# Recurrent mixer: block sums of the weights by accumulating transfers, and heads 0 to 3 scaled in earlier scans

## The chip, the cores and the metric

The kernel runs on one core of one Trainium2 chip. Five engines share the core: TensorE (PE in the profile; PEld is its loading of stationary operands), VectorE (DVE), ScalarE (ACT), GpSimd (POOL) and SyncE (SP), which here only issues transfers. The metric is the device time of one execution in microseconds (us). Before the change it is 2783.34 us, the median of three runs from 2783.18 to 2783.43.

## The reference, cut to what matters

The program is a trunk of two layers over 768 tokens (two requests, 512 and 256 long) with 1024 features, all in fp32. Each layer is `x += 1/2 ffn(norm(x)); x += mixer(norm(x)); x += 1/2 ffn(norm(x))`. The mixer of the first layer is the recurrent one that the change touches; the second layer's is windowed attention. The recurrent mixer, cut to its core:

```python
def hgrn2_mixer(x, w_in, w_o, g_norm, lb):
    q, i, g, f_fw, f_bw = jnp.split(x @ w_in, 5, axis=-1)      # 8 heads of 128
    k_f, logf_f = gates(f_fw, lb[0])
    k_b, logf_b = gates(f_bw, lb[1])
    o_fwd = gla_chunk_scan(q, k_f, i, logf_f)   # S_t = diag(f_t) S_(t-1) + k_t v_t^T, o_t = S_t^T q_t
    o_bwd = rev(gla_chunk_scan(rev(q), rev(k_b), rev(i), rev(logf_b)))
    o = o_fwd + o_bwd
    o = o * lax.rsqrt(jnp.mean(o * o, axis=-1, keepdims=True) + NORM_EPS)   # per head and token
    o = (o * g_norm).reshape(B, T, H * V) * jax.nn.silu(g)
    return o @ w_o
```

Three of its matrix products have 1024 by 1024 weights and matter here: the values `i` ("v"), the gate `g` ("g") and the output product with `w_o` ("o").

## The kernel before, in words

**Products in three parts.** Every fp32 matrix is split into a high and a low half that TensorE can take at its faster type: `hi` is a cast of the value (ACT), `lo` is the value less `hi` (DVE). A product is then three matmuls, hi·hi, hi·lo and lo·hi. A split of a weight thus costs one cast on ACT and one subtraction on DVE (`split`, L175 and L323/L324).

**Block products.** Each of v, g and o is computed as seven products of blocks in place of eight, a scheme of the Strassen kind. The token side gives `b00`, `b10`, `b11` and four mixed factors `t1` to `t4` (`mix`, L418ff: block sums on DVE, L426 to L432). The weight is cut into quarters a11, a12, a21, a22, and needs these sums: a21 += a22, a11 += a21 (called "second"), a12 += a11 ("fourth"), and s3, which is the a21 as loaded plus a11. Product p1 uses a11 as loaded, p2 uses a12 as loaded, p3 the summed a12, p4 a22, p5 the summed a21, p6 the summed a11, and p7 s3. `tok_steps` (L223ff) loads the quarters by the SP queue and makes them ready. A quarter is held in two halves, kp 0 (one tile `wr` of 128x1024) and kp 1 (two tiles `tA` of 128x512). s3 and a21 += a22 are made by `into` (L147), an accumulating transfer on GpSimd's queue, which adds one tile onto another without a compute engine. "second" and "fourth" are `tensor_add`s on DVE, three for each sum (one of 128x1024, two of 128x512). For v and g, whose products come in the order `TOK` = p1, p2, p7, p6, p5, p4, p3, these adds stand ahead of the splits of p6 and p3 (L260); for o, in the order `OUT` = p1, p2, p3, p7, p6, p4, p5, both stand behind the split of p2 (L272). They are pinned to the program's order.

**Stages.** After the first feed-forward part come the value block (542 to 600 us in the trace), eight scans of one head each (about 42 us each, 600 to 938), the rest of the gate block (to 967) and the output block (to 1029). A scan (`hgrn_scan`, L829ff) goes through seven levels. At each one ACT copies the keys into an operand (`kop`, L857), PE makes the score matmuls from it (`scan_scores`, L827), and DVE writes the scores under a mask (L844 to L846) and updates queries and keys (L879, L883). At its end the head's outputs are copied to the value tiles and their sums of squares kept (L932 to L938). `weave` (L715) puts pieces of other PE work between the steps of a scan: chunks of the next heads' projections (evacuated by ACT at L803) and then products of the gate block (L764 is the matmul of all three block products).

**The normalisation.** `rstds` takes a square root on ACT (L1030) and a reciprocal on DVE. The square root is in another table of ACT than its other functions, so ACT loads a table ahead of it and again behind it. `scaled` then multiplies a head's six blocks of 128x128 by these numbers, on ACT (L1078). Before the change `rstds(0, 7)` runs once, when seven scans are done, and the seven heads are scaled during the eighth scan, one head at each level.

**The start of the output block.** `gated` multiplies the scaled outputs by the gate; `turned` transposes them; `mix` makes t1 to t4 from them, and each operand is split by a cast on ACT and a subtraction on DVE. The product p3 of o is evacuated by a copy on ACT (L1140), into tiles that p7 needs; x is loaded back meanwhile, and p2 is added to it on DVE (L1147).

**What sets the order.** The program is written against a tile scheduler. It puts each engine's instructions into a fixed order by its own model of times, unless they are pinned; every engine then takes its list in order, and waits at an instruction whose inputs or buffers are not ready. Eight `w` tiles hold split weights, four `wr` and eight `tA` raw ones, and PSUM has eight banks. A split is started when buffers come free, so its place among PE's products is set by them.

Of the kernel before, what the change touches and what calls it, by code (L numbers as in the profile page):

```python
# [25 lines left out]
HEADS = 8  # L26
# [18 lines left out]
TOK = ("p1", "p2", "p7", "p6", "p5", "p4", "p3")  # L45
TCHAIN = {"p2": "p1", "p4": "p5", "p3": "p7"}
OUT = ("p1", "p2", "p3", "p7", "p6", "p4", "p5")
# [5 lines left out]
class Trunk:  # L53
# [174 lines left out]
    def tok_steps(self, key, srcs, order):  # L228
        nc = self.nc
        flat = lambda t: t.rearrange("p a b -> p (a b)")  # L230

        def fetch(src):
            t = self.wp.tile([P, 1024], F32, tag="wr", name=self.name("wr"), bufs=RAWBUFS)
            nc.sync.dma_start(t.rearrange("p (a b) -> p a b", a=2), src[0])
            parts = [[t], [self.tmp(512), self.tmp(512)]]
            for a, t in enumerate(parts[1]):
                self.last_load = nc.sync.dma_start(t, src[1][:, a, :])
            return parts

        a11, a12, a21, a22 = (fetch(src) for src in srcs)  # L240
        more = self.big([P, 2, 512])
        s3 = [
            [self.wp.tile([P, 512], F32, tag="s3", name=self.name("s3"), bufs=2) for _ in range(2)],
            [more[:, a, :] for a in range(2)],
        ]
        for kp in range(2):
            for a, t in enumerate(s3[kp]):
                self.last_load = nc.sync.dma_start(t, srcs[2][kp][:, a, :])
                self.into(t, a11[0][0][:, a * 512 : (a + 1) * 512] if kp == 0 else a11[1][a])
            for t, u in zip(a21[kp], a22[kp]):  # L250
                self.into(t, u)
        own = {"p1": a11, "p2": a12, "p3": a12, "p4": a22, "p5": a21, "p6": a11, "p7": s3}
        second, fourth = (a11, a21), (a12, a11)
        sums = {"p6": (second,), "p3": (fourth,)} if order == TOK else {}
        behind = {"p2": (second, fourth)} if order == OUT else {}

        def step(name, kp):
            for total, part in sums.get(name, ()):
                for t, u in zip(total[kp], part[kp]):
                    self.tc.keep_in_program_order(nc.vector.tensor_add(t, t, u))  # L260
            hi, lo = self.wtile(), self.wtile()
            at = 0
            for src in own[name][kp]:
                n = src.shape[-1]
                h, l = (t[:, at : at + n] for t in (hi, lo))
                self.split(src, h, l)
                at += n
            view = lambda t: t.rearrange("p (a b) -> p a b", a=2)
            self.staged[(*key, name, kp)] = (view(hi), view(lo), 2)
            for total, part in behind.get(name, ()):  # L270
                for t, u in zip(total[kp], part[kp]):
                    self.tc.keep_in_program_order(nc.vector.tensor_add(t, t, u))  # L272

        return [(2, lambda name=name, kp=kp: step(name, kp)) for name in order for kp in range(2)]

    def stage_next(self):
# [698 lines left out]
    def hgrn(self, lb_row, gn_row, next_row):  # L975
        nc = self.nc
# [4 lines left out]
        heads = [{} for _ in range(HEADS)]  # L981
# [35 lines left out]
        scan = lambda hd: self.hgrn_scan(hd, vs)  # L1017

        def stream():
            for h in range(1, HEADS):  # L1020
                for c in (0, 3, 4):
                    if (h, c) not in LEAD:
                        yield from self.hgrn_chunk(h, heads[h], c, range(2))
                self.hgrn_gates(h, heads[h])
# [3 lines left out]
        def rstds(a, b):  # L1028
            r = rs[:, a:b, :]
            nc.scalar.activation(r, self.hss[:, a:b, :], AF.Sqrt, bias=self.eps, scale=1.0 / P)  # L1030
            nc.vector.reciprocal(r, r)
# [42 lines left out]
        def scaled(first, last):  # L1074
            for b in range(NBLK):
                for h in range(first, last):
                    u = vs[b][:, h * P : (h + 1) * P]
                    nc.scalar.activation(u, u, AF.Copy, scale=rs[:, h, b : b + 1])  # L1078
# [21 lines left out]
        def gate():  # L1100
            need = {"p1": "t3", "p2": "t2", "p7": "t1", "p6": "t4"}
            for at in self.tok_quad(("g",), TOK, TCHAIN, self.ops, evac_g):
                if at[1:] == (HB - 1, 1) and at[0] in need:
                    self.reload_factor(need[at[0]])
                yield at

        feed = itertools.chain(stream(), gate())
        for h in range(HEADS - 1):
            self.weave(scan(heads[h]), feed, 16 if h == 0 else 18)
        rstds(0, HEADS - 1)  # L1110
        self.weave(scan(heads[-1]), feed, 20, also=lambda i: i < HEADS - 1 and scaled(i, i + 1))
        rstds(HEADS - 1, HEADS)
        scaled(HEADS - 1, HEADS)
        for i in range(HB):
# [441 lines left out]
```

## Time and profile before

| | |
|---|---|
| median of 3 runs | 2783.34 us (2783.18 to 2783.43) |
| the profiled execution | 2783.55 us |
| its span, first to last instruction | 2781.6 us |
| mean granted TensorE clock | 0.998 |
| value block, 542.4 to 599.6 us: PE busy | 57.20 of 57.20 |
| scans one to seven, 599.6 to 892.0: PE busy | 291.94 of 292.40 |
| eighth scan, 892.0 to 938.0: PE busy | 43.10 of 46.00 |
| gate block's rest, 938.0 to 967.5: PE busy | 29.50 of 29.50 |
| output block, 967.5 to 1029.0: PE busy | 58.26 of 61.50 |

The stages' rows are from the view that cuts the span into windows. The difference between a window's length and PE's busy time is PE's waiting; busy time at a lower granted clock still counts as busy. Groups of instructions are named by line, engine, operation and tiles (out<-in); the number in brackets behind an instruction is how long its engine stood idle ahead of it, and on whom it waited.

### The profile page before, as it was taken

How to read it: one execution, taken by the hardware profiler on the slowest of the kernel's cores; microseconds unless marked ns; L12 is line 12 of the kernel's file. 1: busy time of each engine (PE TensorE's matmuls, PEld its weight loads, DVE VectorE, ACT ScalarE, POOL GpSimd, SP SyncE). 2: the span in 40 equal slices, each digit the busy share in tenths (PEclk: the TensorE clock that was granted, in tenths of full speed). 3: DMA queues.
4: the chain of work that ended last, by engine and by line, in shares of the span. 5: the costliest groups of instructions: out<-in, count | busy, mean ns of one | idle time of the engine just before them, and what ended most of it. 6: DMA issues, size and time to landing. Idle time of an engine off the chain costs nothing.

```text
span 2781.6 us, 40766 instructions
## 1 busy us (share of the span) xinstructions
PE 2750.1 (99%) x15117; PEld 2555.3 (92%) x15117; DVE 2228.3 (80%) x3825; ACT 1387.6 (50%) x2586; POOL 393.9 (14%) x431
## 2 busy tenths in 40 slices
PE   8999999999999999999999999999999999999998
PEld 8999999989999879999999999999888889999998
DVE  8788788777887888788878887887848878788877
ACT  7344443634445765444445543444458855444443
POOL 2111121100000001211111121111102211211111
PEclk9999999999999999999999999999999999999999
DMA  6554554731121533655444355544422123655443
GB/s 173 128 126 117 126 141 123 244 107 39 39 67 50 173 92 81 147 133 129 117 113 119 81 144 134 124 122 114 129 73 76 45 63 75 146 133 129 117 115 107
DMA packets 337351, 313.41 MB, mean 113 GB/s; under 512 B 12584, under 2 KB 258816, under 8 KB 337152
## 3 DMA queue, kind: packets, MB, share of 16 engines
q1 hardware_dynamic: 296992, 221.81, 27.1%
q0 software_dynamic: 35856, 75.51, 15.0%
q10 hardware_dynamic: 4304, 13.49, 1.3%
q8 instruction: 119, 1.95, 0.3%
q14 instruction: 80, 0.66, 0.1%
HBM read 225.82 MB, written 15.73 MB: 87 GB/s over the span
## 4 chain that ended last, share of the span: by engine, by line
PE 95%; DVE 2%; ACT 2%; DMA 0%; issue 0%; DVEq 0%; ACTq 0%
PE ps L517 42%; PE ps L581 21%; PE ps L319 6%; PE ps L318 6%; PE ps L320 6%; PE ps L764 5%; PE ps L827 3%; PE ps L932 1%; PE ps L1418 1%; PE ps L908 1%; PE ps L389 1%; PE ps L1430 0%; PE ps L1380 0%; PE ps L1381 0%; PE ps L1431 0%; PE ps L1181 0%
## 5 line engine op out<-in xcount | busy, mean ns | idle before, releaser
L517 PE MATMUL ps<-big,w 128*128 128x384 f32 x6720 | 1169.3, 334 | 0.0
L517 PEld LDWEIGHTS ps<-big,w 128*128 128x128 f32 x6720 | 1165.9, 188 | 1.7 <-ACT tA L534 0.2
L208 ACT CAST w<-wr 128x512 fp32r<-128x512 f32 x600 | 416.0, 707 | 682.6 <-PE ps L517 274.2
L581 PE MATMUL ps<-w,big 128*128 128x512 f32 x2520 | 575.6, 389 | 0.0
L581 PEld LDWEIGHTS ps<-w,big 128*128 128x128 f32 x2520 | 472.6, 188 | 97.9 <-DVE x L603 0.3
L209 DVE TENSOR_TENSOR w<-wr,w 128x512 fp32r<-128x512 f32 (+1 forms) x520 | 430.3, 831 | 156.6 <-ACT w L208 140.1
L603 DVE SCALAR_TENSOR_TENSOR x<-ps,x 128x512 f32<-128x512 f32 x468 | 301.9, 683 | 10.1 <-PE ps L320 10.0
L147 POOL DMA_DIRECT2D s<-wr x126 | 110.9, 885 | 1353.5 <-DMA s<-in_ffn_w_dram 410.0
L318 PE MATMUL ps<-big,w 128*128 128x384 f32 x640 | 219.3, 345 | 2.0 <-ACT w L175 1.0
L319 PE MATMUL ps<-big,w 128*128 128x384 f32 x640 | 215.5, 337 | 0.9 <-DVE big L324 0.9
L320 PE MATMUL ps<-big,w 128*128 128x384 f32 x640 | 214.5, 335 | 0.0
L323 ACT CAST big<-tA 128x384 fp32r<-128x384 f32 x296 | 148.0, 513 | 114.3 <-DVE tA L549 36.4
L764 PE MATMUL ps<-w,big 128*128 128x512 f32 x756 | 179.7, 395 | 3.2 <-ACT big L1140 2.6
L764 PEld LDWEIGHTS ps<-w,big 128*128 128x128 f32 x756 | 141.4, 189 | 33.5 <-ACT big L1140 3.5
L324 DVE TENSOR_TENSOR big<-tA,big 128x384 fp32r<-128x384 f32 x296 | 166.2, 572 | 6.6 <-ACT big L323 4.5
L209 POOL TENSOR_TENSOR w<-wr,w 128x512 fp32r<-128x512 f32 x80 | 136.0, 1700 | 187.2 <-ACT w L208 182.8
L147 POOL DMA_DIRECT2D wr<-wr x103 | 90.8, 882 | 459.5 <-DMA wr<-in_ffn_w_dram 175.3
L318 PE MATMUL ps<-w,big 128*128 128x512 f32 x336 | 134.7, 401 | 0.3 <-DVE big L1441 0.2
L215 DVE TENSOR_TENSOR wr<-wr,wr 128x512 f32<-128x512 f32 (+1 forms) x120 | 122.9, 1024 | 14.2 <-issue 10.2
L320 PE MATMUL ps<-w,big 128*128 128x512 f32 x336 | 132.2, 393 | 0.5 <-DVE big L404 0.5
L319 PE MATMUL ps<-w,big 128*128 128x512 f32 x336 | 131.6, 392 | 0.0
L318 PEld LDWEIGHTS ps<-big,w 128*128 128x128 f32 x640 | 119.9, 188 | 3.2 <-ACT w L175 1.3
(219 smaller groups left out, 3471.2 us busy)
## 6 DMA issues: line engine op xcount, KB each, us to landing
wr<-in_ffn_w_dram SPq DMA_DIRECT2D x264, 512.0 KB, 4.0
s<-wr POOLq DMA_DIRECT2D x126, 256.0 KB, 4.9
s<-in_ffn_w_dram SPq DMA_DIRECT2D x120, 256.0 KB, 3.3
wr<-wr POOLq DMA_DIRECT2D x80, 256.0 KB, 3.8
wr<-in_hg_w_in_dram SPq DMA_DIRECT2D x32, 512.0 KB, 3.9
wr<-wr POOLq DMA_DIRECT2D x23, 512.0 KB, 4.6
spill<-x ACTq DMA_DIRECT2D x12, 512.0 KB, 3.9
kept<-big POOLq DMA_DIRECT2D x8, 768.0 KB, 5.4
```

What stands on the lines that cost most here:

```text
L147: self.nc.gpsimd.dma_start(out, src, accum_op=ALU.add)
L208: nc.scalar.copy(h, src)
L209: (eng or nc.vector).tensor_sub(l, src, h.bitcast(F32))
L318: nc.tensor.matmul(out, a[0], b[0], start=first, stop=False)
L319: nc.tensor.matmul(out, a[0], b[1], start=False, stop=False)
L320: nc.tensor.matmul(out, a[1], b[0], start=False, stop=last)
L323: self.nc.scalar.copy(hi, src)
L324: self.nc.vector.tensor_sub(lo, src, hi.bitcast(F32))
L517: self.nc.tensor.matmul(ps, a[x], b[y], start=first and k == 0 and i == 0, stop=k == 3 and i == 2, skip_group_check=True,)
L581: nc.tensor.matmul(ps, a[x], w[y], start=name == chain and kp == 0 and q == 0, stop=kp == 1 and q == 2, skip_group_check=True,)
L603: self.nc.vector.scalar_tensor_tensor(x, ps, c, x, ALU.mult, ALU.add)
L764: nc.tensor.matmul(ps, x[:, sl], y, start=fresh and k == 0 and q == 0, stop=k == 3 and q == 2, skip_group_check=True,)
```

## The change

First, "second" and "fourth" are no longer added on DVE. They become accumulating transfers on GpSimd's queue, for v, g and o alike: a11 += a21 is issued behind the split of p1, and a12 += a11 behind the split of p2, half by half. For o the quarters are also loaded in another order, a21 and a22 ahead of a11 and a12. In all 18 additions on DVE (six for each block product) become 18 transfers.

Second, the normalisation is cut in three. `rstds(0, 4)` runs when four scans are done, and heads 0 to 3 are to be scaled at the levels 1 and 4 of the scans behind it, one head at a time. `rstds(4, 7)` runs when seven are done, and the eighth scan scales heads 4 to 6 only, at its levels 1, 3 and 5. This makes one square root and two table loads more.

```diff
--- before.py
+++ after.py
@@ -237,7 +237,8 @@
                 self.last_load = nc.sync.dma_start(t, src[1][:, a, :])
             return parts
 
-        a11, a12, a21, a22 = (fetch(src) for src in srcs)
+        got = {i: fetch(srcs[i]) for i in ((0, 1, 2, 3) if order == TOK else (2, 3, 0, 1))}
+        a11, a12, a21, a22 = (got[i] for i in range(4))
         more = self.big([P, 2, 512])
         s3 = [
             [self.wp.tile([P, 512], F32, tag="s3", name=self.name("s3"), bufs=2) for _ in range(2)],
@@ -250,14 +251,9 @@
             for t, u in zip(a21[kp], a22[kp]):
                 self.into(t, u)
         own = {"p1": a11, "p2": a12, "p3": a12, "p4": a22, "p5": a21, "p6": a11, "p7": s3}
-        second, fourth = (a11, a21), (a12, a11)
-        sums = {"p6": (second,), "p3": (fourth,)} if order == TOK else {}
-        behind = {"p2": (second, fourth)} if order == OUT else {}
+        behind = {"p1": (a11, a21), "p2": (a12, a11)}
 
         def step(name, kp):
-            for total, part in sums.get(name, ()):
-                for t, u in zip(total[kp], part[kp]):
-                    self.tc.keep_in_program_order(nc.vector.tensor_add(t, t, u))
             hi, lo = self.wtile(), self.wtile()
             at = 0
             for src in own[name][kp]:
@@ -267,9 +263,9 @@
                 at += n
             view = lambda t: t.rearrange("p (a b) -> p a b", a=2)
             self.staged[(*key, name, kp)] = (view(hi), view(lo), 2)
-            for total, part in behind.get(name, ()):
-                for t, u in zip(total[kp], part[kp]):
-                    self.tc.keep_in_program_order(nc.vector.tensor_add(t, t, u))
+            if name in behind:
+                for t, u in zip(*(parts[kp] for parts in behind[name])):
+                    self.into(t, u)
 
         return [(2, lambda name=name, kp=kp: step(name, kp)) for name in order for kp in range(2)]
 
@@ -1106,9 +1102,13 @@
 
         feed = itertools.chain(stream(), gate())
         for h in range(HEADS - 1):
-            self.weave(scan(heads[h]), feed, 16 if h == 0 else 18)
-        rstds(0, HEADS - 1)
-        self.weave(scan(heads[-1]), feed, 20, also=lambda i: i < HEADS - 1 and scaled(i, i + 1))
+            early = (lambda i, h=h: i in (1, 4) and len(ready) and scaled(*ready.pop(0))) if h > 3 else None
+            self.weave(scan(heads[h]), feed, 16 if h == 0 else 18, also=early)
+            if h == 3:
+                rstds(0, 4)
+                ready = [(i, i + 1) for i in range(4)]
+        rstds(4, HEADS - 1)
+        self.weave(scan(heads[-1]), feed, 20, also=lambda i: i in (1, 3, 5) and scaled(4 + i // 2, 5 + i // 2))
         rstds(HEADS - 1, HEADS)
         scaled(HEADS - 1, HEADS)
         for i in range(HB):
```

Below are rows of the engines' orders. A row names the line, the operation and its tiles; the lines of the changed kernel are four lower than those of the kernel before in this part of the code. Names: L938 and L934 are the copies of a head's outputs into the value tiles x, L857 and L853 the key copies, L1078 and L1074 the scalings, `hrs` the reciprocal roots, `ps` a PSUM bank.

ACT at the end of the fourth scan and the start of the fifth, before:

```order
L936 ACTIVATE big_6810<-ps_6859 128x256
L938 COPY x_5093<-ps_6859 128x128
L938 COPY x_5109<-ps_6859 128x128
L857 COPY big_6884<-big_6781 128x768
L175 CAST w_6929<-wr_6401 128x1024
L803 ACTIVATE big_6789<-ps_6848 128x384
```

and after:

```order
L934 COPY x_5115<-ps_6859 128x128
L1026 ACT_TABLE_LOAD
L1026 ACTIVATE hrs<-hss,eps 128x24
L853 COPY big_6886<-big_6781 128x768
L1074 ACTIVATE x_5082<-x_5082,hrs 128x128
L1074 ACTIVATE x_5098<-x_5098,hrs 128x128
L1074 ACTIVATE x_5114<-x_5114,hrs 128x128
L1074 ACTIVATE x_5083<-x_5083,hrs 128x128
L1074 ACTIVATE x_5099<-x_5099,hrs 128x128
L1074 ACTIVATE x_5115<-x_5115,hrs 128x128
```

The square root and its table load now stand between the copies of the fourth head's outputs and the second key copy of the fifth scan, and six scalings follow that copy; all 24 scalings of heads 0 to 3, and the load of the other table, stand in this scan.

ACT in the eighth scan, around the key copy of its fifth level, before:

```order
L1078 ACTIVATE x_5109<-x_5109,hrs 128x128
L1078 ACTIVATE x_5076<-x_5076,hrs 128x128
L1078 ACTIVATE x_5092<-x_5092,hrs 128x128
L1078 ACTIVATE x_5108<-x_5108,hrs 128x128
L857 COPY big_7990<-big_7893 128x768
L1078 ACTIVATE x_5077<-x_5077,hrs 128x128
L1078 ACTIVATE x_5093<-x_5093,hrs 128x128
L323 CAST w_8183<-tA_7395 128x512
```

and after (L1041 evacuates a product of the gate block, L319 and L323 are casts of weights for it):

```order
L319 CAST w_8157<-wr_7413 128x1024
L1074 ACTIVATE x_5082<-x_5082,hrs 128x128
L319 CAST w_8200<-tA_7415 128x512
L1041 ACTIVATE big_8108<-ps_8051 128x512
L319 CAST w_8200<-tA_7416 128x512
L1074 ACTIVATE x_5098<-x_5098,hrs 128x128
L853 COPY big_8022<-big_7925 128x768
L1074 ACTIVATE x_5114<-x_5114,hrs 128x128
L1074 ACTIVATE x_5083<-x_5083,hrs 128x128
```

Ahead of this key copy there stood a run of scalings; now there are casts of weights, with two scalings among them and two behind.

DVE at the start of the output block, before (L324 are splits of weights, L272 the additions "second" and "fourth", L426 and L427 the first block sums, L1147 an addition of p2 to x):

```order
L324 TENSOR_TENSOR w_8709<-wr_8314,w_8708 128x1024
L272 TENSOR_TENSOR wr_8308<-wr_8308,wr_8320 128x1024
L324 TENSOR_TENSOR w_8715<-tA_8316,w_8714 128x512
L272 TENSOR_TENSOR wr_8314<-wr_8314,wr_8308 128x1024
L324 TENSOR_TENSOR w_8715<-tA_8317,w_8714 128x512
L272 TENSOR_TENSOR tA_8310<-tA_8310,tA_8322 128x512
L272 TENSOR_TENSOR tA_8311<-tA_8311,tA_8323 128x512
L272 TENSOR_TENSOR tA_8316<-tA_8316,tA_8310 128x512
L272 TENSOR_TENSOR tA_8317<-tA_8317,tA_8311 128x512
L426 TENSOR_TENSOR big_8577<-big_8746,big_8577 128x768
L1147 TENSOR_TENSOR x_8678<-ps_8724,x_8678 128x512
L427 TENSOR_TENSOR big_8746<-big_8481,big_8746 128x768
```

and after:

```order
L320 TENSOR_TENSOR w_8714<-wr_8331,w_8713 128x1024
L320 TENSOR_TENSOR w_8719<-tA_8333,w_8718 128x512
L320 TENSOR_TENSOR w_8719<-tA_8334,w_8718 128x512
L422 TENSOR_TENSOR big_8579<-big_8748,big_8579 128x768 x2
L423 TENSOR_TENSOR big_8748<-big_8486,big_8748 128x768 x2
L426 TENSOR_TENSOR big_8486<-big_8486,big_8579 128x768 x2
L428 TENSOR_TENSOR big_8656<-big_8656,big_8486 128x768
L1147 TENSOR_TENSOR x_8683<-ps_8726,x_8683 128x512
```

The six additions are gone from between the splits of p2 (its a12 as loaded is `wr_8314`, `tA_8316`, `tA_8317` before and `wr_8331`, `tA_8333`, `tA_8334` after), and the block sums follow the last of these splits directly. The additions are found again on POOL, as the last transfers of the mixer:

```order
L147 DMA wr_8325<-wr_8313 128x1024
L147 DMA tA_8327<-tA_8315 128x512
L147 DMA tA_8328<-tA_8316 128x512
L147 DMA wr_8331<-wr_8325 128x1024
L147 DMA tA_8333<-tA_8327 128x512
L147 DMA tA_8334<-tA_8328 128x512
```

In these `wr_8325`, `tA_8327` and `tA_8328` are a11, to which a21 is added; `wr_8331`, `tA_8333` and `tA_8334` are a12, to which that sum is added, so that each of the last three rows waits for one of the first three.

## The prediction

> **What bounds the kernel now.** I read the profile's page first: busy time by engine, and the chain that ended last.
>
> ```profile
> PE 2750.1 (99%) x15117; PEld 2555.3 (92%) x15117; DVE 2228.3 (80%) x3825; ACT 1387.6 (50%) x2586; POOL 393.9 (14%) x431
> ...
> PE 95%; DVE 2%; ACT 2%; DMA 0%; issue 0%; DVEq 0%; ACTq 0%
> ```
>
> TensorE (PE) is busy 2750.1 of 2781.6 us, so work taken off VectorE (DVE) or ScalarE (ACT) counts only where PE waits. Next I read PE's waits in the recurrent mixer: the window 890 to 1000 us (last scan, gate block, start of the output block), then, in the last row, 540 to 892 (value block, scans one to seven). A row says who waited for whom: us in total, times, longest.
>
> ```profile
> PE ps L764 <- ACT big L1140: 2.6, 2, 2.3
> PE ps L827 <- ACT big L857: 1.9, 1, 1.9
> PE ps L827 <- DVE big L879: 0.7, 1, 0.7
> PE ps L764 <- DVE w L324: 0.6, 1, 0.6
> PE ps L908 <- ACT big L901: 0.2, 1, 0.2
> ...
> PE ps L932 <- DVE big L919: 0.4, 1, 0.4
> ```
>
> In the 350 us ahead of the last scan PE waits 0.4 us, so what is removed there gains nothing. All there is to win stands in five rows, 6.0 us; the timeline places four of them.
>
> ```profile
> 907.94 1.58 PE L827 MATMUL ps<-big,big 128*128 128x128 f32 x12 [0.71 <-DVE big L879]
> 914.22 1.60 PE L827 MATMUL ps<-big,big 128*128 128x128 f32 x12 [1.95 <-ACT big L857]
> 988.17 6.19 PE L764 MATMUL ps<-w,big 128*128 128x512 f32 x26 [0.63 <-DVE w L324]
> 996.66 1.21 PE L764 MATMUL ps<-w,big 128*128 128x512 f32 x4 [2.30 <-ACT big L1140]
> ```
>
> Two lie in the eighth scan, two where the output block starts. The last has a sequel that the waits don't show. In these windows the columns are length, PE busy (count), granted clock, DMA share, GB/s:
>
> ```profile
> 995.33:998.74 3.41, 1.77 (x6) 1.00 0.27 77
> 998.74:1002.15 3.41, 3.41 (x9) 0.50 0.33 92
> ```
>
> After 3.41 us in which PE was busy only 1.77, the next 3.41 us ran at half clock: half of them, 1.7 us, were lost.
>
> **The change, part by part.** *Scaling removed from the eighth scan.* ACT before the 1.95 us wait:
>
> ```profile
> 910.39 3.04 ACT L1078 ACTIVATE x<-x,hrs 128x128 f32<-128x128 f32 x10
> 913.33 0.83 ACT L857 COPY big<-big 128x768 f32<-128x768 f32 x1
> ```
>
> The key copy (L857) that PE waits for stands behind ten scalings, 0.30 us each. Of 42 scalings in this scan 18 stay; between this copy and the one before it the order had 15 and now has six, so the copy comes some 2.7 us earlier, and PE's score matmuls, which wait for nothing else of ACT's, with it. The third level's scores move up by 14 matmuls of the gate block, so part of that slack is spent; I take 2.5 of the 0.71 + 1.95 = 2.66 us as gained (ends: 0, if the waits form again at other levels; 2.66).
>
> *Scaling added to the fifth scan.* 24 scalings, a square root and two table loads land in its first half. ACT and the score matmuls there, and a table load:
>
> ```profile
> 766.21 0.91 ACT L857 COPY big<-big 128x768 f32<-128x768 f32 x1 [0.40 <-ACT x L938]
> 769.93 1.05 ACT L175 CAST w<-wr 128x1024 fp32r<-128x1024 f32 x1 [2.81 <-PE ps L319]
> ...
> 773.15 0.84 ACT L857 COPY big<-big 128x768 f32<-128x768 f32 x1 [1.78 <-issue]
> 775.74 0.49 ACT L803 ACTIVATE big<-ps 128x384 f32<-128x384 f32 x1 [1.75 <-PE ps L320]
> 777.12 0.84 ACT L857 COPY big<-big 128x768 f32<-128x768 f32 x1 [0.89 <-PE ps L827]
> 781.58 0.84 ACT L857 COPY big<-big 128x768 f32<-128x768 f32 x1 [3.62 <-PE ps L827]
> ...
> 771.47 1.60 PE L827 MATMUL ps<-big,big 128*128 128x128 f32 x12
> 775.54 1.50 PE L827 MATMUL ps<-big,big 128*128 128x128 f32 x12
> 780.00 1.50 PE L827 MATMUL ps<-big,big 128*128 128x128 f32 x12
> ...
> 894.30 1.28 ACT L1030 ACT_TABLE_LOAD   x1
> 895.60 0.33 ACT L1030 ACTIVATE hrs<-hss,eps 128x42 f32<-128x42 f32 x1
> ```
>
> Added: 24 x 0.30 + 2 x 1.28 + 0.33 = 10.1 us; ACT's idle time in this stretch: 0.40 + 2.81 + 1.78 + 1.75 + 0.89 + 3.62 = 11.25. It must fit level by level. Second level: 1.28 + 0.33 ahead of the copy that ends at 767.12, scores at 771.47: 4.35 of slack. Third: 13 scalings, 3.9 us, into 2.81 + 1.78 = 4.6 idle. Fourth: six scalings and a load, 3.1 us, into 1.75 + 0.89 = 2.6: 0.5 late, where the copy ends at 777.96 and scores start at 780.00, 2.0 of slack. Fifth: five scalings, 1.5, into 3.62. Cost: 0, hidden by ACT's idle time (ends: 0; 10.1 if none of it hid).
>
> Here the Trainium skill speaks against the change: its page "ScalarE Activation LUTs", section What ACT_TABLE_LOAD costs, gives about 1380 ns of drain beside each load's 1283. The rows show no drain: the square root starts 1.30 us after the load. By that page of the Trainium skill two switches would add 2.8 us, and the fourth level would be 1.9 us late against 2.0 of slack: 2776.5 us by either, with the margin nearly gone by the Trainium skill.
>
> *Additions off VectorE.* 18 leave:
>
> ```profile
> L260 DVE TENSOR_TENSOR tA<-tA,tA x8: 682/684/690, 562.3 to 955.8; 128x512 f32<-128x512 f32 x8
> L260 DVE TENSOR_TENSOR wr<-wr,wr x4: 1216/1220/1220, 552.8 to 952.3; 128x1024 f32<-128x1024 f32 x4
> ...
> 974.66 2.49 DVE L272 TENSOR_TENSOR tA<-tA,tA 128x512 f32<-128x512 f32 x4
> 977.07 0.95 DVE L426 TENSOR_TENSOR big<-big,big 128x768 f32<-128x768 f32 x1
> ...
> 987.43 0.68 DVE L324 TENSOR_TENSOR w<-tA,w 128x512 fp32r<-128x512 f32 x1
> ...
> 993.58 0.95 DVE L432 TENSOR_TENSOR big<-big,big 128x768 f32<-128x768 f32 x1
> ...
> 974.30 0.57 ACT L1091 ACTIVATE big<-ps,cols 128x384 f32<-128x384 f32 x1
> ...
> 996.03 0.58 ACT L1140 COPY big<-ps 128x512 f32<-128x512 f32 x1
> ```
>
> With the output block's six (2 x 1.22 + 2.49) that is 15.3 us of VectorE, nearly all where PE never waited. The output block's six count. The block sums (L426 to L432) start at 977.07, though the first one's input was there at 974.87. In a run an operation costs some 0.08 less than alone (2.49 for four, 0.684 for one). Started at 974.87, seven sums of 0.87 end at 981.0; the addition to x (0.6), the eighth sum (0.87), product three's first weight split (1.14), four operand splits of 0.87 and its second split (2 x 0.6) follow in the new order: 988.3, against 988.11 now. So the 0.63 us wait stays. But all eight sums are done by 982.4, where now the last ends at 994.5; ACT's operand casts wait for them, and product three's evacuation (L1140) stands behind those casts at 996.03, though its matmuls end near 988.17 + 12 x 0.24 = 991.0. That wait, 2.6 us in two pieces, goes, and with it the half clock, 1.7 us (ends: 0; 2.6 + 0.6 + 1.7 = 4.9).
>
> Of the clock the Trainium skill says ("TensorE: Matmul & The Clock Gate", section What's actually happening) that it halves after at least one idle window of about 3.4 us. The rows contradict that page of the Trainium skill: 1.64 us idle in one window was enough. By the Trainium skill this half clock had another cause and would stay, and the sum would be 1.7 us less of a gain: 2778.2 by it, 2776.5 by the rows.
>
> *Transfers added.* 18 accumulating transfers on GpSimd's queue (POOL), about 0.9 us of issue each (1.79 for two, below): 16 us on an engine busy 14%. Queued behind their waits are the spills of the factors and the mask conversion; PE waits for neither in the value block. There and in the gate block the sums are started two products or more ahead of products six and three. Tight is the output block alone: a21+=a22, a11+=a21, a12+=a11, then product three. The nearest rows, the end of product one's split, and two casts:
>
> ```profile
> tA<-tA POOLq DMA_DIRECT2D x2, 256.0 KB, 8.0
> ...
> 963.85 1.79 POOL L147 DMA_DIRECT2D tA<-tA  x2 [0.51 <-DMA tA<-in_hg_w_o_dram]
> ...
> 963.53 1.28 DVE L324 TENSOR_TENSOR w<-tA,w 128x512 fp32r<-128x512 f32 x2
> ...
> DMA to landing us min/median/max: 5.4/6.0/9.0
> ...
> 922.77 1.13 ACT L323 CAST w<-tA 128x512 fp32r<-128x512 f32 x2
> ```
>
> a11+=a21 can issue when product one is split, at 964.8; the second of its pair lands at 964.8 + 1.8 + 8.0 = 974.6, and a12+=a11 at 984.4 (ends for a transfer: 5.4 and 9.0, the last row but one, which is of loads). VectorE reaches these weights at 987.1 in the new order and ACT needs 1.13 us for them first, so landing by 986.0 costs nothing: margin 1.6 us. Behind ACT's waiting cast stand the last operand casts and L1140. The SP queue loads a21 and a22 first now; a11 comes third, behind the split of gate product four instead of five, about 36 x 0.24 = 8.6 us later, and its own split is two products further on.
>
> Sum: 2.5 + 2.6 + 1.7 = 6.8 us less. The profiled execution took 2783.55 us, 1.95 more than its span and 0.2 more than the median, 2783.34; against the median that is **2776.5 us**, 0.24% faster.
>
> **The rivals.**
> 1. *The sums land late.* At 9.4 us instead of 8.0 for two steps in a row a12+=a11 lands at 987.2, and product three's split ends near 989.6 (1.13 and 2 x 0.6 later) instead of 988.3; the wait at 988 grows by 1.3, L1140 follows late, and the window of low activity comes again. Gained then: the scan's 2.5 and some 0.5: 2780.3. For it: the x reloads share the engines in just these us. Against it: 1.6 us of margin.
> 2. *The eighth scan's waits form again*, since scores move up and VectorE orders the key products later: 2.6 + 1.7 gained, 2779.0. For it: slack under 1 us at two levels. Against it: 24 fewer scalings.
> 3. *The half clock stays.* If it hangs on how many matmuls ran in the few us ahead, and not on the wait, the output block's start keeps it: 6.8 - 1.7 = 5.1 us gained, 2778.2. For it: PE still waits some 0.6 us at product three. Against it: it begins right behind the 2.30 us wait, and not at the start of the block's products. The Trainium skill's rule on idle windows (the section above) points the same way.
> 4. *Slower: ACT in the fifth scan doesn't fit.* If the 10.1 us don't hide in idle time, key copies come after their scores are due, and PE waits there instead: 2783.3 - 6.8 + 10.1 = 2786.6. It decides from 6.8 us of new waits on. Against it: the level-by-level fit above.
>
> **How the numbers follow.** Forecast 0.56, its own range 2775.0 to 2778.0; rivals 0.17, 0.12, 0.08, 0.07. The range goes down to 2775.0: all 6.0 us of waits and the half clock gone (2775.6), and 0.6 for slow restarts behind the waits, which no row prices. It goes up to 2781.5, which takes in rivals 1 to 3. A measurement of this kernel tells about 0.2% (5.6 us) from no change: faster by more (under 2777.8) is the forecast but for its upper edge, 0.54; slower is rival 4, 0.07; the rest, 0.39, is within.
>
> **What would show it.** Right: no PE wait over 0.5 us in the last scan; the L1140 wait gone and granted clock 1.00 behind it; a wait of 0.3 to 1 us at product three; no PE wait in the fifth scan. Wrong: PE waiting on the key copy in the fifth scan (rival 4), ACT or POOL waiting for accumulating transfers around 980 us with PE behind them (rival 1), a half-clock window near 1000 us with no wait ahead of it (rival 3).

## The result, and the profile after

The changed kernel takes 2774.59 us, the median of 7 runs (2774.10 to 2775.27); the kernel before took 2783.34 beside it (7 runs, 2781.87 to 2783.97). The ratio is 0.9969, with a 95% interval of 0.9959 to 0.9980: 8.75 us or 0.31% faster. The forecast was 2776.5 within 2775.0 to 2781.5, so the sign and the places were right, and the time lies 0.4 us below the range. The profiled execution took 2774.57 us.

The page's busy times, and PE's waits in the windows 890 to 1000 us and then 540 to 892, as the prediction read them:

```profile
PE 2747.2 (99%) x15117; PEld 2554.7 (92%) x15117; DVE 2220.5 (80%) x3808; ACT 1389.7 (50%) x2589; POOL 410.5 (15%) x449
...
PE ps L904 <- ACT big L897: 0.2, 1, 0.2
...
PE ps L928 <- DVE big L915: 0.4, 1, 0.4
```

Of the five rows of waits, 6.0 us, only the smallest, 0.2 us, is left. In the same stage windows as in the table above (length, PE busy and count, then the other engines, granted clock, DMA share, GB/s):

```profile
599.60:892.00 292.40, 291.96 (x2030) 288.18 (x2029) 234.75 (x409) 136.30 (x253) 9.57 (x11) 1.00 0.21 52
892.00:938.00 46.00, 45.76 (x275) 40.29 (x274) 39.01 (x73) 30.15 (x69) 2.61 (x3) 1.00 0.62 205
938.00:967.50 29.50, 29.48 (x148) 24.30 (x147) 22.24 (x31) 24.31 (x43) 6.14 (x7) 1.00 0.71 163
967.50:1029.00 61.50, 60.84 (x289) 50.44 (x288) 51.24 (x74) 42.76 (x74) 4.76 (x5) 1.00 0.46 123
```

PE is busy 45.76 of 46.00 us in the eighth scan (43.10 before), and the output block's window now holds 289 matmuls instead of 254 at clock 1.00 instead of 0.97: the feed-forward part that follows starts inside it. (The window ends at 1029.00; the output block's last matmul started at 1032.83 before the change and starts at 1024.07 now.)

For all that follows, two lengths are worked out from the start times of the block products' matmuls (L764 in the kernel before) in each profiled execution: A, from the first matmul of the gate block to its last (the eighth scan lies within), and B, from the output block's first to its last. Before, A was 88.87 and B 65.43; after, 85.56 and 60.08. So 3.31 us came from A and 5.35 from B. Of the 9.1 us between the two spans (2781.6 and 2772.5 us), the other 0.5 lies in stretches that the change leaves alone; the profiled executions of the runs below differ among themselves there by more (1.4 us ahead of the value block alone, 541.35 to 542.76).

ACT in the fifth scan, where the prediction had summed 10.1 us of added work level by level:

```profile
765.71 1.28 ACT L1026 ACT_TABLE_LOAD   x1
767.00 0.32 ACT L1026 ACTIVATE hrs<-hss,eps 128x24 f32<-128x24 f32 x1
767.22 0.91 ACT L853 COPY big<-big 128x768 f32<-128x768 f32 x1
768.04 2.16 ACT L1074 ACTIVATE x<-x,hrs 128x128 f32<-128x128 f32 x7
...
773.90 1.87 ACT L1074 ACTIVATE x<-x,hrs 128x128 f32<-128x128 f32 x6
775.79 1.28 ACT L799 ACT_TABLE_LOAD   x1
777.08 0.49 ACT L799 ACTIVATE big<-ps 128x384 f32<-128x384 f32 x1
777.47 0.82 ACT L853 COPY big<-big 128x768 f32<-128x768 f32 x1
778.20 1.57 ACT L1074 ACTIVATE x<-x,hrs 128x128 f32<-128x128 f32 x5
```

All of it hides: PE has no wait from 764 us to the one of 0.4 us in a later scan's end, which was there before. The key copy behind the second table load ends at 778.29; the prediction's sum for it was 778.46. The instruction behind a load starts 1.29 us after the load does, and the second load starts 0.02 us behind the end of the scalings ahead of it (775.77). So the drain of about 1380 ns that the Trainium skill gives ("ScalarE: Activation LUTs", section What ACT_TABLE_LOAD costs) isn't in these rows, on either side of the load.

ACT in the output block, around the evacuation of product three (L1140) for which PE had waited:

```profile
978.34 0.62 ACT L319 CAST w<-tA 128x512 fp32r<-128x512 f32 x1
979.48 0.62 ACT L319 CAST w<-tA 128x512 fp32r<-128x512 f32 x1 [0.52 <-DMA tA<-tA]
980.00 3.04 ACT L319 CAST big<-big 128x768 fp32r<-128x768 f32 x4
982.95 1.13 ACT L319 CAST w<-s 128x512 fp32r<-128x512 f32 x2
985.03 0.59 ACT L1140 COPY big<-ps 128x512 f32<-128x512 f32 x1 [0.95 <-PE ps L760]
```

L1140 now waits for PE and not the other way round. The last tile of a12 += a11 lands at 979.48, where ACT has waited 0.52 us for it.

### The profile page after: what moved, and what is told of

Its sections match the earlier page's. It is cut to its first block, busy times and chain, and to the rows that moved or that the text cites. A ratio compares the mean times of both kernels' runs of the same rounds, so it can differ in the third digit from the quotient of the medians.

```text
span 2772.5 us, 40790 instructions
## 1 busy us (share of the span) xinstructions
PE 2747.2 (99%) x15117; PEld 2554.7 (92%) x15117; DVE 2220.5 (80%) x3808; ACT 1389.7 (50%) x2589; POOL 410.5 (15%) x449
## 3 DMA queue, kind: packets, MB, share of 16 engines
q8 instruction: 119, 1.95, 0.3%
## 4 chain that ended last, share of the span: by engine, by line
PE 95%; DVE 2%; ACT 1%; DMA 0%; issue 0%; DVEq 0%; ACTq 0%; SPq 0%
PE ps L513 42%; PE ps L577 21%; PE ps L315 6%; PE ps L314 6%; PE ps L316 6%; PE ps L760 5%; PE ps L823 3%; PE ps L928 1%; PE ps L1418 1%; PE ps L904 1%; PE ps L385 1%; PE ps L1430 0%; PE ps L1380 0%; PE ps L1381 0%; PE ps L1431 0%; PE ps L1181 0%
## 5 line engine op out<-in xcount | busy, mean ns | idle before, releaser
L209 DVE TENSOR_TENSOR w<-wr,w 128x512 fp32r<-128x512 f32 (+1 forms) x520 | 437.8, 846 | 147.5 <-ACT w L208 131.5
L319 ACT CAST big<-tA 128x384 fp32r<-128x384 f32 x296 | 148.0, 513 | 113.4 <-DVE tA L552 36.2
```

The costliest lines, as they stand in the source:

```text
L209: (eng or nc.vector).tensor_sub(l, src, h.bitcast(F32))
L319: self.nc.scalar.copy(hi, src)
```

## The experiments

Each run stands beside the kernel before on the same chip, whose median was 2782.99 beside e1 to e4, 2782.89 beside e5 to e8, 2783.25 beside e9 to e11 and 2783.37 beside e12.

### Each half of the change alone

Run e1, the scaling alone (the kernel before with the second part of the change):

```diff
-            self.weave(scan(heads[h]), feed, 16 if h == 0 else 18)
-        rstds(0, HEADS - 1)
+            early = (lambda i, h=h: i in (1, 4) and len(ready) and scaled(*ready.pop(0))) if h > 3 else None
+            self.weave(scan(heads[h]), feed, 16 if h == 0 else 18, also=early)
...
+        rstds(4, HEADS - 1)
```

> Only the scaling is moved (heads 0 to 3 normalised behind the fourth scan); all weight sums stay on VectorE. Theory M (ScalarE's scalings were what the eighth scan waited for; each wait of PE costs some 0.26 us more than the wait row says): the two waits of the eighth scan go and nothing else, 0.71 + 1.95 + 2 x 0.3 = 3.3 us, 2783.3 - 3.3 = 2780.0; the waits for L1140 (2.6 us) and for the weight split at product three (0.6 us) stay, and so does the window at clock 0.50 behind them. Rival R1 (the eighth scan's waits went because VectorE lost the gate block's additions): under 1 us gained, 2782.5 or more, with the key-copy wait still there.

Measured: 2780.68 us, ratio 0.9990 (0.9981 to 0.9999). A is 87.13, 1.74 us shorter, where 3.3 was expected; B is 64.89, 0.5 shorter. PE's waits, 540 to 1035 us:

```profile
PE ps L764 <- ACT big L1144: 2.3, 1, 2.3
PE ps L764 <- DVE w L324: 0.6, 1, 0.6
PE ps L827 <- ACT big L857: 0.5, 2, 0.3
...
PE ps L827 <- DVE big L879: 0.3, 1, 0.3
```

The wait of 1.95 us went, but three of 0.2 to 0.3 us formed in its place: the prediction's second rival, in part. ACT stands idle 2.93 us for VectorE, which is adding g's quarters, and 3.02 for PE, with the next key copy behind both in its order:

```profile
908.51 0.84 ACT L857 COPY big<-big 128x768 f32<-128x768 f32 x1
909.25 0.41 ACT L1078 ACTIVATE x<-x,hrs 128x128 f32<-128x128 f32 x1
912.59 1.22 ACT L323 CAST w<-tA 128x512 fp32r<-128x512 f32 x2 [2.93 <-DVE tA L260]
916.83 1.06 ACT L323 CAST w<-wr 128x1024 fp32r<-128x1024 f32 x1 [3.02 <-PE ps L764]
917.78 0.83 ACT L857 COPY big<-big 128x768 f32<-128x768 f32 x1
```

Run e2, the sums alone (transfers for v, g and o, all seven heads scaled in the eighth scan as before):

```diff
-        second, fourth = (a11, a21), (a12, a11)
-        sums = {"p6": (second,), "p3": (fourth,)} if order == TOK else {}
-        behind = {"p2": (second, fourth)} if order == OUT else {}
+        behind = {"p1": (a11, a21), "p2": (a12, a11)}
```

> Only the sums are moved to accumulating transfers (v, g and o, with the other load order for o); all seven heads are scaled in the eighth scan as before. Theory M: the output block gains all of its 5.4 us (waits of 2.6 and 0.6, half clock 1.7, restarts 0.5), the eighth scan nothing: 2777.9, with the 0.7 and 1.9 us waits of the scan still there. Rival R1: the scan's waits shrink too, 2775 to 2776.

Measured: 2778.18 us, ratio 0.9981 (0.9972 to 0.9990). B is 60.03, the whole of its gain. A is 87.87, 1.0 us shorter: the scan's two waits became one, of 1.9 us for the key copy (PE L823 <- ACT L853). So the scan's gain has two sources, ScalarE's scalings and VectorE's additions for g: 1.74 and 1.0 us alone, and 3.31 together, 0.6 more than their sum.

### The sums, product by product

Run e3, transfers for o alone:

```diff
+        moved = order == OUT
...
+        behind = {"p1": second, "p2": fourth} if moved else {}
+        sums = {"p6": (second,), "p3": (fourth,)} if order == TOK and not moved else {}
```

> Transfers for the output product o alone; v and g are added on VectorE, scaling as before. Theory M: VectorE's block sums move up, so the L1140 wait and the half clock go (2.6 + 1.7 + 0.3 = 4.6); the 0.6 us wait at product three may stay, since the transposes ahead of the block sums stand where they stood: 2778.7 (2777.9 if it goes too). Rival R2 (the gain came from the gate block's additions leaving VectorE, which let the transposes come earlier): under 1.5 us gained, 2782 or more.

Measured: 2785.91 us, ratio 1.0011 (1.0002 to 1.0019), slower than before. Neither theory had this. PE's waits, and ACT where product three's weights are due:

```profile
PE ps L771 <- ACT w L330: 2.6, 1, 2.6
PE ps L834 <- ACT big L864: 1.9, 1, 1.9
PE ps L771 <- DVE w L331: 1.8, 2, 1.1
...
978.59 0.60 ACT L1143 ACTIVATE big<-ps 128x512 f32<-128x512 f32 x1 [0.78 <-PE ps L771]
988.26 1.04 ACT L330 CAST w<-wr 128x1024 fp32r<-128x1024 f32 x1 [9.07 <-DMA wr<-wr]
```

ACT waits 9.07 us for a12 += a11 and PE behind it: the first rival of the prediction, sums that land late, here in full. B is 68.92, 3.5 us longer than before, and A 90.53, 1.7 longer; the execution in the profile was the slowest of the eleven (2789.01 us), with four half-clock windows in these two stages where the kernel before has one, so the median's 2.9 us is the better measure of the loss. The transfers are the same as in the changed kernel, and so is the load order; what differs is when the loads are issued. SP's queue in this run, and in the changed kernel: the first load of o (a21), and as the last row the third, that of a11:

```profile
926.72 0.38 SPq L234 DMA_DIRECT2D wr<-in_hg_w_o_dram  x1
930.76 0.93 SPq L237 DMA_DIRECT2D tA<-in_hg_w_o_dram  x2
...
954.99 0.38 SPq L234 DMA_DIRECT2D wr<-in_hg_w_o_dram  x1
```

```profile
907.98 0.38 SPq L234 DMA_DIRECT2D wr<-in_hg_w_o_dram  x1
910.87 1.10 SPq L237 DMA_DIRECT2D tA<-in_hg_w_o_dram  x2
...
932.77 0.38 SPq L234 DMA_DIRECT2D wr<-in_hg_w_o_dram  x1
```

Without g's transfers the first load of o is issued 18.7 us later (in e2, with them, at 909.17), and that of a11 22.2 us later. Run e4 does the other part:

```diff
+        moved = order == TOK
```

> Transfers for v and g alone; the output product's sums stay on VectorE, scaling as before. Theory M: PE never waits in those stretches and the output block's additions still hold the block sums up: 0 to 0.9 us gained, 2782.4 to 2783.3, with the L1140 wait and the half clock still there. Rival R2: 3 us or more gained, under 2780.3.

Measured: 2783.17 us, ratio 0.9999 (0.9990 to 1.0008). B is 65.33, as before; A is 87.91, 1.0 shorter. So v's and g's transfers alone bring nothing that the time shows, o's alone cost 2.9 us, and together (e2) they bring 4.8: one is the other's condition.

### Why o's transfers need g's

The loads of o wait for `wr` buffers that g lets go. In e3 the first two are let go by the splits of g's products five and four (the loads are issued 0.02 to 0.03 us behind the ends of these splits, 926.70 and 937.54). The third, that of a11, waits for the buffer of g's a11. The last to read that is the addition a12 += a11, which stands ahead of product three, the last of the seven. With g's transfers, long landed by then, the last to read it is the split of product six, the fourth. So its buffer is let go first, every load of o moves up by one place, and that of a11 comes behind the split of product four. The addition in e3, and then the first part of a11 += a21 in e3 and in the changed kernel:

```profile
953.74 1.22 DVE L263 TENSOR_TENSOR wr<-wr,wr 128x1024 f32<-128x1024 f32 x1
...
968.99 0.86 POOL L147 DMA_DIRECT2D wr<-wr  x1 [0.81 <-DMA big<-tA]
```

```profile
957.91 0.86 POOL L147 DMA_DIRECT2D wr<-wr  x1 [12.15 <-DVE w L320]
```

The load is issued at 954.99, 0.03 us behind the end of the addition. In e3 the sum waits for the transfer that makes s3, which needs a11 too, and then takes 10.1 us to land; in the changed kernel it waits for the split of product one, and takes 5.2. If the late release is the cause, VectorE may keep g's additions, provided that the second one comes earlier. Run e6 is e3 with that:

```diff
-        sums = {"p6": (second,), "p3": (fourth,)} if order == TOK and not moved else {}
+        sums = {"p6": (second, fourth)} if order == TOK and not moved else {}
```

> The run with transfers for o alone, and one thing more: v's and g's additions stay on VectorE, but a12 += a11 stands ahead of product six beside a11 += a21, not ahead of product three. Theory T (with the addition ahead of product three, g's a11 is read until the gate block's end, so its buffer comes free 18 us late, o's first load starts at 927 instead of 908 us, and the sums land late): the first load of o starts near 909, no engine waits for an accumulating transfer around 985, the output block takes 60 to 61 us instead of 68.9: 2777.5 to 2779. Rival R2 (what v's and g's transfers give the output block is VectorE's time or another order of the transposes): the waits for the transfers stay, 2783 or more.

Measured: 2780.99 us, ratio 0.9993 (0.9985 to 1.0002). SP's queue, and PE's waits:

```profile
911.25 0.38 SPq L234 DMA_DIRECT2D wr<-in_hg_w_o_dram  x1
...
938.04 0.38 SPq L234 DMA_DIRECT2D wr<-in_hg_w_o_dram  x1
...
PE ps L834 <- ACT big L864: 4.5, 2, 3.1
PE ps L834 <- DVE big L886: 0.7, 1, 0.7
```

The first load comes at 911.25 and that of a11 at 938.04, no engine waits for a sum, and B is 60.05. That is theory T for the output block, though the load that counts is a11's and not the first. The whole time missed its range, since A is 91.74, 2.9 longer than before: in this run ACT's order has 14 scalings in a row (4.21 us) ahead of the key copy for which PE waits 3.1. Run e7 has the scaling moved as well:

> The same with the scaling of heads 0 to 3 moved as in the change: all of the change but v's and g's sums, which stay on VectorE. Theory T: the output block as in the changed kernel; the eighth scan keeps the short waits that the run with the scaling alone has, since VectorE still adds g's quarters there (1.7 us gained of 3.3): 2783.0 - 5.4 - 1.7 = 2775.9, some 1.3 above the changed kernel. Rival (g's additions on VectorE cost the scan nothing): 2774.6.

Measured: 2777.01 us, ratio 0.9979 (0.9970 to 0.9988). B is 60.07 and A 88.07, 0.8 shorter than before where 1.7 was expected. What g's transfers give over additions in the right place is the scan, 2.5 us. Run e12 is the changed kernel with v's sums alone back on VectorE (`moved = key != ("v",)`):

> The changed kernel, but v's two sums stay on VectorE; g and o by transfers, scaling moved. Theory T (only g's transfers, by the early release of their buffers and by VectorE's time in the eighth scan, and o's count; in the value block PE never waits): 2774.5, the same as the changed kernel, with the first load of o near 908, scan and gate block 85.5 us and output block 60.1 us. Rival (v's sums matter too, since their buffers pass on to g's loads and so to o's): g's and o's loads come late, 2776 or more.

Measured: 2774.40 us, ratio 0.9969 (0.9958 to 0.9980), A 85.55, B 60.05: v's six transfers do nothing for the time.

### The other parts of the change

Run e5, o's load order as before:

```diff
-        got = {i: fetch(srcs[i]) for i in ((0, 1, 2, 3) if order == TOK else (2, 3, 0, 1))}
+        got = {i: fetch(srcs[i]) for i in range(4)}
```

> The changed kernel, but the quarters of o are loaded in the order a11, a12, a21, a22 as before the change. Theory T (the sums' landing decides, and a sum can start only when its quarters are loaded): a21 += a22 has to wait for the last load (near 950 us instead of 925), so a12 += a11 lands some 4 to 8 us later than the 979.5 us of the changed kernel, later than ScalarE's cast of product three takes it; PE waits 1 to 4 us at product three and a half-clock window may follow: 2776 to 2781. Rival (the load order is of no matter, 3 us of room cover it): 2774.6.

Measured: 2774.48 us, ratio 0.9970 (0.9959 to 0.9982): no difference. The rival was right. a11 += a21 was issued at 957.82 here and at 957.91 in the changed kernel, since in both it waits for the split of product one and not for a load.

Run e8, the changed kernel without o's transfers, with o's additions on VectorE:

> The changed kernel, but o's two sums stay on VectorE behind the split of product two, and its loads in the old order: scaling moved, v and g by transfers. Theory T: the eighth scan gains all of its 3.3 us, since neither ScalarE's scalings nor VectorE's additions for g are in it; the output block keeps its waits for L1140 and the weight split (0.1 to 0.5 gained): 2779.1 to 2779.6. Rival (the scan's waits re-form for other reasons): 2781 or more.

Measured: 2779.54 us, ratio 0.9986 (0.9978 to 0.9995). A is 85.54, the whole gain of the scan, and B 64.87, 0.6 shorter than before. A and B can thus be won apart: what e8 gains in A and e2 in B add up to 8.7 us.

### What a wait costs, and when the clock halves

To make waits of known lengths, runs e9 to e11 repeat the subtraction of product three's first weight split, which delays that product and leaves the result as it is (one repeat is shown):

```diff
                 self.split(src, h, l)
+                if order == OUT and (name, kp) == ("p3", 0):
+                    for _ in range(1):
+                        nc.vector.tensor_sub(l, src, h.bitcast(F32))
```

> The changed kernel with one repeat of the first weight split's subtraction for product three of o (1.14 to 1.22 us of VectorE right ahead of that product; the result is the same). Theory W (a wait costs its length, and halves the clock of the next window of 3.413 us only where PE stands idle for about 2 us or more of one window): a wait of some 1.3 us at product three, no half-clock window behind it in any execution, 2774.5 + 1.2 = 2775.7. Rival H (the output block's start lowers the clock by itself as soon as a wait of about 1 us stands there): 2777.4.

> Two repeats. Theory W: a wait of some 2.5 us; it holds 2 us of one window in about half of the executions, since the windows' grid lies differently in each: times in two groups near 2776.9 and 2778.5, the median between them. Rival F (only a window that is idle throughout halves the clock): one group near 2776.9, clock 1.00 behind the wait. The Trainium skill's page on TensorE and its clock gate, section What's actually happening, has it as rival F does.

> Four repeats. Theory W: a wait of some 4.8 us, which always leaves more than 2 us idle in one window, so the half clock follows in every execution: 2774.5 + 4.7 + 1.7 = 2780.9. Rival F: a wait of 4.8 us holds a whole window of 3.41 us in (4.8 - 3.41) / 3.41 = 4 of 10 executions; median near 2779.2, with single times of 2780.9.

Measured, with one, two and four repeats: 2775.38, 2775.85 and 2781.89 us (ratios 0.9970, 0.9972 and 0.9993, the last from 0.9984 to 1.0001). The waits came out as 0.4 us, 1.0 and 0.2, and 5.0: the scheduler put the work around the repeats in another order, so e10 has no wait of 2.5 us and doesn't separate W from F. Its wait of 1.0 us has the clock at 1.00 behind it, against rival H; e9 has no wait of that length. With four repeats B is 66.34, 6.26 longer: 5.0 for the wait and 0.3 for the restart behind it, some 1.6 for one half-clock window, less the 0.4 that stood there, 6.5 in all. Windows on the grid of the clock in e11, and then in e6, where PE waits 3.1 us in one piece:

```profile
979.55:982.97 3.42, 2.15 (x10) 1.46 (x8) 3.42 (x4) 3.42 (x6) 0.00 (x0) 1.00 0.00 0
982.97:986.38 3.41, 0.00 (x0) 0.00 (x0) 3.41 (x4) 0.83 (x2) 0.00 (x0) 1.00 0.00 0
986.38:989.79 3.41, 3.10 (x7) 2.49 (x8) 3.41 (x6) 0.60 (x1) 0.00 (x0) 0.50 0.51 150
```

```profile
909.17:912.58 3.41, 2.12 (x10) 1.41 (x8) 3.41 (x5) 3.41 (x12) 0.00 (x0) 1.00 0.09 11
912.58:915.99 3.41, 1.61 (x13) 1.61 (x14) 3.41 (x8) 3.41 (x10) 0.00 (x0) 1.00 0.38 143
915.99:919.41 3.42, 3.42 (x16) 2.79 (x16) 3.42 (x6) 0.86 (x3) 0.00 (x0) 1.00 0.34 112
```

The wait of 3.1 us, split by the grid's edge at 912.58, left the clock alone. In e3 one of 1.9 us that lay within a window halved it, so a window needn't be idle throughout:

```profile
911.45:914.87 3.42, 1.50 (x10) 1.04 (x9) 3.42 (x7) 3.42 (x11) 0.00 (x0) 1.00 0.01 4
914.87:918.28 3.41, 3.41 (x13) 2.93 (x12) 3.41 (x7) 2.78 (x9) 0.00 (x0) 0.50 0.00 0
```

PE's idle time in a window can be counted more sharply than by busy time, by the distance from each matmul's start to the next less what it is in a run (0.227 us for 512 columns, 0.111 for 128). In the traces that have a half-clock window ahead of the kernel's end, by which the grid can be fixed (before, e1 to e4, e6, e8, e11 and e12), each of the 17 windows with about 2.05 us or more of idle time was followed by one at 0.50, and none of those with less than about 1.95 was; the first 9 us and the end are left out. The count is good to some 0.1 us, and in a window that runs at 0.50 itself (two of the 17) it takes slower matmuls for idle time. In the kernel before, the two waits for L1140 (2.3 and 0.3 us) left 2.06 in one window. The grid starts at another place in each execution (2.05, 1.94, 0.59, 0.10, 0.21 us into the span in the first five), so the same wait halves the clock in one execution and not in another: the wait of 1.9 us for the key copy stands in before, e2, e3 and e4, and has a half-clock window behind it in e3 alone. The rule of the Trainium skill ("TensorE: Matmul & The Clock Gate", section What's actually happening), that it takes an idle window of about 3.4 us, is not what these rows show. All 11 executions with four repeats lie between 2780.31 and 2783.18, none near the 2779.2 that was worked out for such a rule.

## Why the prediction was right or wrong, point by point

**Where the time is won: right.** Two places, the eighth scan and the start of the output block, by the waits named; PE, not VectorE, is the bound.

**The sum: too small by 2 us, and this is the step that failed.** The terms were 2.5 + 2.6 + 1.7 = 6.8. Measured by A and B they are 3.31 and 5.35. Two things were mis-sized. First, each wait was priced at its row, and the range's lower end allowed 0.6 us in all for "slow restarts behind the waits, which no row prices". The start times of matmuls in the trace of before do price them: across the 1.95 us wait they are 2.11 us further apart than in a run, and the next one comes 0.10 late; across the others 0.88 + 0.07 for 0.71, 0.79 + 0.11 for 0.63, and 2.46 + 0.11 and 0.48 + 0.11 for L1140's two. That is 7.2 us for 5.9 in the rows: 0.27 more for each of the five. The eighth scan's two make 3.2 of the 3.31 measured. Second, "the 0.63 us wait stays" was wrong: by the starts of the matmuls 0.31 + 0.11 is left in the changed kernel of 0.90 before, with an idle gap too short for the view of waits. VectorE's block sums began 6.6 us after the output block's start, and not 7.5, which the prediction had taken over from before (974.87 less 967.39), because the last eight of the twelve transposes ahead of them now stand earlier in PE's order (before: four, five matmuls, eight; now: eight, one matmul, four); its work ended that much sooner. What moved the transposes was not tested. The output block is then 3.2 (L1140) + 0.5 + 1.6 (half clock, eight distances of 0.20) = 5.3.

**"I take 2.5 of 2.66": too careful in the changed kernel, right as a doubt.** The scan's waits did form again when the scaling alone was moved.

**"In the 350 us ahead of the last scan ... what is removed there gains nothing": right.** v's sums are worth nothing, and the added ACT work in the fifth scan costs nothing; there is no sign of rival 4.

**"Additions off VectorE ... the output block's six count": wrong.** g's six count too, 1.0 us alone and 1.6 beside the scaling, as additions in the eighth scan.

**The landing of the sums: tight, as it said, with the condition missed.** The prediction had a11 += a21 issued at 964.8, where product one's split ends before the change, and a12 += a11 landed at 984.4, with 1.6 us to spare. Its place for the load of a11, behind the split of gate product four and some 8.6 us after 925.30, was right (932.77). But it didn't say that this place exists only because g's transfers let go of g's a11 three products sooner. Product one's split came earlier as well: the sums issue from 957.91 and have landed at 979.5. By the prediction's own working they need not be there before 982.6 (986.0 less the 3.4 that the block starts earlier), which is an estimate. Without g's transfers rival 1 is what happens, as e3 shows, and worse than priced: 2.9 us lost, where the rival left 0.5 of the output block's gain.

**The half clock: right.** It stands behind the L1140 wait of 2.3 us in the four profiles that have that wait (before, e1, e4, e8), and is gone where no wait of such a length took its place. Its price, 1.7, was 1.6; that it depends on the grid's place in the execution was not seen.

## What to carry to other kernels

Where one engine is at 99%, price a wait from the distances between its instructions' starts, not from the wait's row: here each cost 0.27 us more, and the longest another 1.6 by the clock in the execution that was profiled. When a sum or a copy moves to another queue, ask first which buffer its old place held, and until when: the transfers of the output product were worth 5.0 us (e2 against e4) or minus 2.9 (e3), by where the product ahead of it let go of one tile. Parts of a change can be each other's condition, so each alone is no measure of its share.

## What the runs showed of the hardware that was not expected

The granted clock is set in windows of 3.413 us on a grid that lies differently in each execution; about 2 us of idle time within one window halve the next, and 3.1 us across an edge did not. In the attention stage such a window came and went between executions (2183.2 us before, none after) with the stage's length at 177.3 us in both (from the first matmul of L1380 to the last of L1430), so a half clock needn't cost anything. Accumulating transfers between tiles took a median of 5.3 us for 512 KB and 8.4 for 256 KB from 900 to 1000 us of the changed kernel, the smaller the longer.
